# Moving one held store from GpSimd's queue to SyncE's, and counting with sixteen semaphores in place of thirty-six

## The chip, the cores and the metric

The kernel runs on one core of a Trainium2 chip. The metric is the device time of one execution in microseconds; the median of several executions is given, and beside it one execution that was profiled. The core's engines each run their own list of instructions: PE is TensorE (matrix products and transposes; PEld its weight loads), DVE is VectorE, ACT is ScalarE, POOL is GpSimd, SP is SyncE. They meet only through semaphores: an instruction can wait until a semaphore has reached a value, and can add to one when it is done. Transfers between the device memory and the core's on-chip memory are issued by GpSimd (queue q0, software_dynamic) or by SyncE (queue q1, hardware_dynamic), and are carried out by 16 DMA engines. A transfer adds 16 to its semaphore when all of it has landed. PSUM is the memory that TensorE writes, in eight banks.

## The reference

For each of 8 x 12 heads, a 1024 x 1024 matrix of weights is multiplied with a 1024 x 64 matrix:

```python
batch, n_heads, seq, head_dim = 8, 12, 1024, 64
attn_weights = np.random.randn(batch, n_heads, seq, seq).astype(np.float32)
v = np.random.randn(batch, n_heads, seq, head_dim).astype(np.float32)
return np.einsum('bhqs,bhsd->bhqd', attn_weights, v).astype(np.float32)
```

The weights are 403 MB in fp32, v and the output 25 MB each.

## The kernel before

**Units.** The 96 heads are taken four at a time (NV = 24 quartets, numbered q), and each quartet in two units (NU = 48, numbered n), each with half of the rows of the weights. A unit's weights are loaded in one transfer by GpSimd (`load_attn`, L340), which turns fp32 into bf16 on the way: 4 MB land in one of two buffers `abf`. The last two units' loads are cut into two halves each. v is loaded by GpSimd in a few larger pieces (`load_v`, L348), except for one part that SyncE loads at the start (L133).

**A unit on TensorE** (`pe_unit`, L198). It waits for its load, then transposes 16 groups g of the weights (`transpose_g`, L138, four matrix instructions each) into four PSUM banks in turn; group g goes to bank g % 4, and from g = 4 on has to wait until the copy of group g - 4 has emptied the bank. At g = 8 it also waits on `s_half`. In the first unit of a quartet it then spreads v over the partitions (`spread_v`, L153). `transpose_back` (L170) turns the products of the unit before; then come the products of this unit, 64 matrix instructions in two parts (`multiply`, L183), behind a wait on `s_last` for the last copies (L221).

**VectorE and ScalarE** (`engine`, L241, once for each). They share the 16 copies of the transposed groups out of PSUM (`copy_g`, L274: groups with g % 8 in 0, 2, 4, 5, 7 on VectorE, the others on ScalarE), the copies of spread v (`spread_copy`, L247), and the copies of the products into `ot` (`product`, L285). The copies of what was turned back into the output buffer `osb` (`back_copies`, L267) are ScalarE's, except for half of the last ones, which is VectorE's. A loop of 12 passes handles four units in each; the counts that a copy waits for are sums of a base in a register and a constant.

**GpSimd's list** (L365 to L402). Two loads at the start, two fills of constants (`affine_select`, L370 and L381), then for each unit n: wait until TensorE has transposed unit n's last group, then issue the load of unit n + 2 into the freed buffer (L395, L396). Behind the first units of quartets 8 and 16, it issues stores of finished output (`BURSTS`, L398: quartets 0 to 7, 8 and 9, 10 to 13). Then come the *held* stores (L400): quartets 14 and 15, 16 and 17, 18 and 19, one store of 2 MB for each pair, issued behind the last load in the same queue. Last stands `pool.drain()` (L402).

**SyncE's list** (L408 to L429). It relays landings to other engines: it waits for a burst or a load of v, then raises `s_free`, `s_half` or `s_vr`. At the end it waits for each of the two second half loads (L424), raising `s_half` (L425), then issues the store of quartets 20 and 21 (L427), waits until the last two copies into `osb` are done (`s_fin`, L428), and issues the last store, quartets 22 and 23 (L429).

**The end.** ScalarE, behind its copies, waits until GpSimd's held stores have landed (L335). All engines then meet (L135 in the profile: GpSimd gives the sign when it is through its list), ScalarE waits until SyncE's stores have landed (L432) and adds to the semaphore (L433), and the program clears its semaphores and ends (L459 in the profile).

**Semaphores.** There are 36: among them one for each of the groups 0 to 11 (`s_cp`, L125), `s_last` for groups 14 and 15, and for TensorE's work five: two for the transposes (`s_t`, by the engine that copies them), `s_sp` for spread v, `s_back` for what was turned back, `s_m` for the products.

Of the kernel before, what the change touches and what calls it, by code (L numbers as in the profile page):

```python
# [10 lines left out]
def kernel(  # L11
# [27 lines left out]
    VH = 4  # L39
# [14 lines left out]
    BY_SYNC = NV - 4  # L54
# [33 lines left out]
    def count_of(g):  # L88

        return sum(on_dve(x) == on_dve(g) for x in range(g + 1))  # L90

    PER_DVE = sum(on_dve(g) for g in range(G))
    PER_ACT = G - PER_DVE

# [40 lines left out]
    with tc.tile_critical(sync_engine=mybir.EngineType.Pool, no_gpsimd_drain=True):  # L135
        pe = nc.tensor

        def transpose_g(a, g, n):  # L138
            if g >= 4:
                pe.wait_ge(s_cp[g - 4], n)  # L140
            words = a[:, g].bitcast(fp32).rearrange("p (c k) -> p k c", k=KW)
            for k in range(KW):
                last = pe.matmul(  # L143
                    out=pt[g % 4][:, k],
                    lhsT=words[:, k],
                    rhs=ident,
                    is_transpose=True,
                    start=(k == 0),
                    stop=(k == KW - 1),
                )  # L150
            last.then_inc(s_t[on_dve(g)])

        def spread_v(n, banks):  # L153

            for pair in ((0, 2), (1, 3)):
                for b in range(VB):
                    for h in pair:
                        j = n % 2 * VH + h
                        rows = ds(j * (P // V8) // VR * VR, VR)
                        last = pe.matmul(  # L160
                            out=banks[h],
                            lhsT=spread[rows, j, ds(VB - 1 - b, P)],
                            rhs=vr[rows, n // 2, b],
                            start=(b == 0),
                            stop=(b == VB - 1),
                        )
                        if b == VB - 1:
                            last.then_inc(s_sp)

        def transpose_back():  # L170
            for j0 in range(0, GH, 4):
                for j in range(4):
                    last = pe.matmul(  # L173
                        out=px[j0 // 4][:, ds(j * P, P)],
                        lhsT=ot[:, j0 + j],
                        rhs=ident,
                        is_transpose=True,
                        start=(j == 0),
                        stop=(j == 3),
                    )  # L180
                last.then_inc(s_back)
# [16 lines left out]
        def pe_unit(i, n, both, loaded, it):  # L198

            pe.wait_ge(*loaded)  # L200
            for g in range(G):
                if g == GH:
                    pe.wait_ge(s_half, n)
                transpose_g(abf[i], g, n)
            pe.wait_ge(s_ot, both)
            if i == 0:
                pe.wait_ge(s_vr, it)
# [12 lines left out]
            transpose_back()  # L220
            pe.wait_ge(s_last, both)  # L221
            for hp in range(2):
                for h in range(2):
                    for half in range(2):
                        outs = po[hp][ds(half * D, D), ds(h * GH * VP, GH * VP)]
                        last = multiply(outs, 2 * hp + h, half)
                last.then_inc(s_m)

        pe.wait_ge(s_const, 4)
        with nc.Fori(1, NV + 1, 1, engines=(PE,)) as it:  # L230
# [4 lines left out]
            pe_unit(0, first, pe.snap(both - 2), (s_abf[0], loaded), it)  # L235
            pe_unit(1, second, both, (s_abf[1], loaded), it)
        pe.wait_ge(s_ot, 2 * (NU + 1))
# [3 lines left out]
        def engine(dve):  # L241
            eng = nc.vector if dve else nc.scalar
            copy = nc.vector.tensor_copy if dve else nc.scalar.copy
            per = PER_DVE if dve else PER_ACT
            e = 0 if dve else 1

            def spread_copy(h, ps, count):  # L247
                eng.wait_ge(s_sp, count)
                copy(  # L249
                    out=vbf[:, :, h], in_=ps.rearrange("p (k d) -> p k d", k=SB)  # L250
                ).then_inc(s_vbf)

            def back_copy(rows, n, k, count):

                eng.wait_ge(s_back, count)
                for pp in range(2):
                    last = copy(  # L257
                        out=rows[ds(n // 2 % 2 * HP, HP), ds(pp * 2 * G + n % 2 * G, G)].rearrange(
                            "p (half j) d -> p j half d", half=2
                        )[:, ds(4 * k, 4)],  # L260
                        in_=px[k][ds(pp * HP, HP)].rearrange(
                            "p (j half d) -> p j half d", half=2, d=D
                        ),
                    )
                return last

            def back_copies(rows, n, count, free=None):  # L267
                if free is not None:
                    eng.wait_ge(s_free, free)
# [4 lines left out]
            def copy_g(g, count):  # L274
                eng.wait_ge(s_t[dve], count)
                ins = copy(  # L276
                    out=at[:, g].rearrange("c k j two -> c (k j two)"),
                    in_=bank[g % 4].bitcast(bf16),
                )
                if g < G - 4:  # L280
                    ins.then_inc(s_cp[g])
                elif g == (G - 1 if dve else G - 2):
                    ins.then_inc(s_last)

            def product(count):  # L285

                eng.wait_ge(s_m, count)
# [7 lines left out]
            def unit(n, base, rows, free):  # L295

                of_t, of_sp, of_back, of_m = base
                for g in mine:
                    copy_g(g, of_t + (n * per + count_of(g)))
                if n % 2 == 0:  # L300
                    spread_copy(e, po[e], of_sp + (2 * n + 2 * e + 2))
                    spread_copy(2 + e, px[e], of_sp + (2 * n + 2 * e + 2))
                if not dve:
                    back_copies(rows, (n - 1) % un, of_back + 2 * n, free)
                product(of_m + (2 * n + e + 1))
# [3 lines left out]
            with nc.Fori(1, NU // un + 1, 1, engines=(DVE if dve else ACT,)) as it:  # L309
                base = [eng.snap(it * (un * k) - un * k) for k in (per, 2, 2, 2)]  # L310
# [3 lines left out]
                else:  # L314
                    now = eng.snap((it - 1) % (NO // 2))
                    before = eng.snap((it + (NO // 2 - 2)) % (NO // 2))
                    free = eng.snap(it + 0)
# [4 lines left out]
            back_copy(osb[:, slot(NV - 1)], NU - 1, k, 2 * NU + k + 1).then_inc(s_fin)  # L322

        nc.vector.memset(ident, 0.0).then_inc(s_const)  # L324
        nc.vector.memset(spread, 0.0).then_inc(s_const)
# [6 lines left out]
        last.then_inc(s_cast)  # L332
        engine(True)
        engine(False)
        nc.scalar.wait_ge(s_held, 16 * (BY_SYNC - HELD_FROM) // 2)  # L335
# [4 lines left out]
        def load_attn(n):  # L340
            pieces = [(0, G)] if n < HALVED else [(0, GH), (GH, GH)]
            for g0, gn in pieces:
# [3 lines left out]
                ).then_inc(s_abf[n % 2] if g0 == 0 else s_second[n], 16)  # L346
# [15 lines left out]
        def store_2(q):  # L362
            store(q, 2, pool, s_held)

        load_attn(0)  # L365
        pool.dma_start(out=vr_first[:, 1], in_=v_first[:, 1]).then_inc(s_v0, 16)
        load_attn(1)
        tc.wait_critical_data_deps()
        pool.wait_ge(s_const, 2)
# [8 lines left out]
        ).then_inc(s_const)  # L378

        pool.wait_ge(s_const, 3)  # L380
# [8 lines left out]
        ).then_inc(s_const)  # L389
        for n in range(NU - 2):  # L390
            q, i = n // 2, n % 2
            if i == 0 and q + 1 in V_LOADS:
                pool.wait_ge(s_sp, 4 * (q + 1))
# [14 lines left out]
        nc.sync.sem_inc(s_free, NO // 2)  # L408
        nc.sync.sem_inc(s_half, WHOLE[0])
        nc.sync.wait_ge(s_cast, 1)  # L410
        nc.sync.wait_ge(s_v0, 16)
        nc.sync.sem_inc(s_vr, 2)
        for k in range(1, NV // 2):
            stored = 2 * (k - 1)
            if stored in BURSTS:
                done = list(BURSTS).index(stored)
                nc.sync.wait_ge(s_osb, 16 * sum(len(BURSTS[x]) for x in BURSTS if x <= stored))
                nc.sync.sem_inc(s_free, sum(fours for _, fours in BURSTS[stored]) // 2)
                nc.sync.sem_inc(s_half, WHOLE[done + 1])  # L419
            if 2 * k in V_LOADS:  # L420
                nc.sync.wait_ge(s_v, 16 * (1 + list(V_LOADS).index(2 * k)))
# [9 lines left out]
        nc.scalar.reg_mov(landed, 16 * 2)  # L431
# [32 lines left out]
```

## Time and profile before

| | us |
|---|---|
| median of 3 runs | 1054.05 |
| lowest and highest of them | 1053.57, 1055.65 |
| the profiled execution | 1053.05 |
| its span, from the first to the last instruction | 1051.3 |
| mean granted clock of TensorE in it | 0.871 of full speed |

In the profile, times count from the start of the span. An engine's busy time leaves out what only its sequencer does: register instructions, branches, waits, the issuing of transfers; such rows carry a q (POOLq, SPq). A row of a group gives the line of the kernel, the engine, the operation, what is written and read, the count, then busy time, mean duration in ns and idle time before it. A row that asks for one line's instructions gives the shortest, median and longest duration in ns, then the first and last start in us. A row of waits gives who waited for whom: us in total, how often, the longest.

### The profile page before, as it was taken

To read this page: it belongs to the slowest core of one execution; us is meant where nothing else is said; L and a number is where in the kernel's file an instruction comes from. 1 tells how busy PE (TensorE), PEld (TensorE's weight loads), DVE (VectorE), ACT (ScalarE), POOL (GpSimd) and SP (SyncE) were. 2 spreads that over 40 slices of the span, in tenths; PEclk is the share of its full clock that TensorE was granted. 3 is DMA by queue.
4 is the path that set the end of the run, shared out by engine and by line. 5 is a ranking of instruction groups with operands and counts; after the bars stand their busy time and mean duration, and the time that the engine had idled before them with its cause. 6 is when DMAs were issued, how large, how long until landed. Compare 5 with 4: busy or idle time off the path is not lost.

```text
span 1051.3 us, 17364 instructions
## 1 busy us (share of the span) xinstructions
PE 796.3 (76%) x7304; PEld 709.4 (67%) x7304; DVE 389.5 (37%) x584; ACT 469.9 (45%) x590; POOL 37.4 (4%) x69
## 2 busy tenths in 40 slices
PE   0877788479889493878939789749588894978993
PEld 0776687468778483767838688648567784867873
DVE  1443344234435141343514344324334341534442
ACT  0445355244545251454626355434335443544552
POOL 1000000000000000000000000000000000000100
PEclk9989799698989697888969899878878987988997
DMA  9999999999999999999999999999999999999998
GB/s 215 225 218 218 216 217 209 219 219 219 217 218 214 218 211 379 219 219 216 215 217 213 216 219 219 209 226 218 330 217 216 219 210 225 218 216 216 211 231 369
DMA packets 10662, 239.68 MB, mean 228 GB/s; under 512 B 1056, under 2 KB 1056, under 8 KB 1184
## 3 DMA queue, kind: packets, MB, share of 16 engines
q0 software_dynamic: 10224, 234.36, 99.2%
q1 hardware_dynamic: 432, 5.24, 1.2%
q8 instruction: 3, 0.05, 0.0%
q14 instruction: 3, 0.02, 0.0%
HBM read 427.82 MB, written 25.17 MB: 431 GB/s over the span
## 4 chain that ended last, share of the span: by engine, by line
DMA 71%; PE 26%; issue 1%; POOL 1%; ACT 0%; DVE 0%; ACTq 0%; SPq 0%; POOLq 0%
DMA abf<-in_attn_weights_dram 63%; PE bank L143 22%; DMA out_dram<-osb 8%; PE bank L160 3%; PE bank L188 1%; PE bank L173 0%; POOL vr L349 0%; ACT osb L257 0%; DVE osb L257 0%; ACT vbf L249 0%; POOL abf L343 0%; ACT ot L288 0%; POOL out_dram L357 0%; ACTq L257 0%; SPq L419 0%
## 5 line engine op out<-in xcount | busy, mean ns | idle before, releaser
L143 PE MATMUL bank<-ident,abf 128*128 128x128 f32 x3072 | 431.5, 308 | 209.7 <-DMA abf<-in_attn_weights_dram 185.7
L143 PEld LDWEIGHTS bank<-ident,abf 128*128 128x128 f32 x3072 | 421.9, 212 | 221.4 <-DMA abf<-in_attn_weights_dram 193.0
L276 DVE COPY at<-bank 128x1024 bf16<-128x1024 bf16 x480 | 319.7, 689 | 401.0 <-PE bank L143 395.7
L276 ACT COPY at<-bank 128x1024 bf16<-128x1024 bf16 x288 | 288.0, 1013 | 327.8 <-PE bank L143 327.8
L188 PE MATMUL bank<-at,vbf 128*64 128x256 bf16 x3072 | 225.6, 285 | 0.0
L188 PEld LDWEIGHTS bank<-at,vbf 128*64 128x64 bf16 x3072 | 203.5, 111 | 19.4 <-issue 6.3
L257 ACT COPY osb<-bank 64x512 f32 (+1 forms) x194 | 112.5, 580 | 28.4 <-PE bank L173 25.7
L288 DVE COPY ot<-bank 128x512 f32<-128x512 f32 x48 | 33.2, 692 | 208.1 <-PE bank L188 208.1
L160 PE MATMUL bank<-vr,spread 32*128 32x512 bf16 x768 | 87.0, 375 | 0.5 <-issue 0.3
L288 ACT COPY ot<-bank 128x512 f32<-128x512 f32 x48 | 28.1, 586 | 129.7 <-PE bank L188 129.7
L173 PE MATMUL bank<-ident,ot 128*128 128x128 f32 x392 | 62.2, 311 | 29.4 <-ACT vbf L249 28.7
L173 PEld LDWEIGHTS bank<-ident,ot 128*128 128x128 f32 x392 | 51.1, 159 | 41.4 <-ACT vbf L249 40.5
L160 PEld LDWEIGHTS bank<-vr,spread 32*128 32x128 bf16 x768 | 35.0, 93 | 44.0 <-issue 1.6
L249 ACT CAST vbf<-bank 128x512 bf16<-128x512 f32 x48 | 25.8, 589 | 74.3 <-PE bank L160 74.3
L343 POOL DMA_DIRECT2D abf<-in_attn_weights_dram x50 | 26.9, 537 | 814.7 <-PE bank L143 813.8
L249 DVE CAST vbf<-bank 128x512 bf16<-128x512 f32 x48 | 30.9, 686 | 29.0 <-PE bank L160 29.0
L276 ACT ACT_TABLE_LOAD x12 | 15.4, 1283 | 6.6 <-DMA osb<-in_v_dram 6.5
L349 POOL DMA_DIRECT2D vr<-in_v_dram x6 | 4.0, 674 | 134.3 <-PE bank L160 134.3
L357 POOL DMA_DIRECT2D out_dram<-osb x6 | 3.6, 604 | 7.6 <-ACT osb L257 7.6
L324 DVE MEMSET ident<- 128x128 f32 x1 | 0.2, 165 | 6.4 <-DMA osb<-in_v_dram 6.4
L257 DVE COPY osb<-bank 64x512 f32<-64x512 f32 x2 | 1.4, 690 | 3.0 <-PE bank L173 3.0
L331 DVE CAST vr<-osb 128x1024 bf16<-128x1024 f32 x2 | 2.2, 1138 | 0.0
(9 smaller groups left out, 5.1 us busy)
## 6 DMA issues: line engine op xcount, KB each, us to landing
abf<-in_attn_weights_dram POOLq DMA_DIRECT2D x46, 4096.0 KB, 28.9
vr<-in_v_dram POOLq DMA_DIRECT2D x5, 2048.0 KB, 15.7
out_dram<-osb POOLq DMA_DIRECT2D x1, 8192.0 KB, 39.6
out_dram<-osb POOLq DMA_DIRECT2D x4, 2048.0 KB, 37.1
abf<-in_attn_weights_dram POOLq DMA_DIRECT2D x4, 2048.0 KB, 23.0
out_dram<-osb POOLq DMA_DIRECT2D x1, 4096.0 KB, 41.7
out_dram<-osb SPq DMA_DIRECT2D x2, 2048.0 KB, 12.9
osb<-in_v_dram SPq DMA_DIRECT2D x1, 1024.0 KB, 5.3
```

The costliest lines, as they stand in the source:

```text
L143: last = pe.matmul(out=pt[g % 4][:, k], lhsT=words[:, k], rhs=ident, is_transpose=True, start=(k == 0), stop=(k == KW - 1),)
L160: last = pe.matmul(out=banks[h], lhsT=spread[rows, j, ds(VB - 1 - b, P)], rhs=vr[rows, n // 2, b], start=(b == 0), stop=(b == VB - 1),)
L173: last = pe.matmul(out=px[j0 // 4][:, ds(j * P, P)], lhsT=ot[:, j0 + j], rhs=ident, is_transpose=True, start=(j == 0), stop=(j == 3),)
L188: last = pe.matmul(out=outs, lhsT=vbf[:, 2 * kw + par, h], rhs=at[:, ds(half * GH, GH), kw, ds(h * VP, VP), par], start=(n == 0), stop=(n ...
L249: copy(out=vbf[:, :, h], in_=ps.rearrange("p (k d) -> p k d", k=SB)).then_inc(s_vbf)
L257: last = copy(out=rows[ds(n // 2 % 2 * HP, HP), ds(pp * 2 * G + n % 2 * G, G)].rearrange("p (half j) d -> p j half d", half=2)[:, ds(4 * k ...
L276: ins = copy(out=at[:, g].rearrange("c k j two -> c (k j two)"), in_=bank[g % 4].bitcast(bf16),)
L288: copy(out=ot.rearrange("c j (pp h p) -> c h j pp p", pp=2, h=VH)[:, ds(2 * e, 2)], in_=po[e].rearrange("c (h j p pp) -> c h j pp p", h=2, ...
L331: last = nc.vector.tensor_copy(out=vr_first[:, 0, part], in_=v32[:, part])
L343: pool.dma_start(out=abf[n % 2][:, ds(g0, gn)].rearrange("p g s -> p (g s)"), in_=attn_q[n // 2][:, ds((n % 2 * G + g0) * S, gn * S)],).th ...
L349: pool.dma_start(out=vr[:, ds(q % V_AT_ONCE // 2, fours // 2)].rearrange("p n b x -> p n (b x)"), in_=v_n(q, fours),).then_inc(s_v, 16)
L357: eng.dma_start(out=out_n(q, fours), in_=at_slot, **({"single_packet": True} if eng is pool and fours == 2 else {}),).then_inc(done, 16)
```

## The change

- `BY_SYNC` is NV - 6 in place of NV - 4, and SyncE's one store behind the half loads becomes a loop. So the held store of quartets 18 and 19 is issued by SyncE, ahead of that of 20 and 21. Its landing counts on `s_end`, for which ScalarE now waits for three stores at the very end.
- GpSimd's held stores (now two) count on `s_osb`, the semaphore of the bursts, and GpSimd waits for the bursts before it issues them.
- One semaphore `s_pe` counts all that TensorE finishes in program order: transposed groups, spread v, what was turned back, products. `event` and `back_event` give the count at which something is done; a pair of units has EV = 44 such events.
- Each bank of the transposes has a semaphore (`s_bank`), which every copy out of it raises; TensorE waits for the count of that bank, held in registers, and before the products for all four banks.
- The remaining semaphores are merged in the same way: constants and VectorE's first cast count on `s_ot` and `s_vr`, the last copies on `s_vbf`, the freeing of output slots on `s_half`, the first load of v and the second half of unit 46's load on `s_v`.
- GpSimd's second fill of constants no longer waits for the first.

```diff
-    BY_SYNC = NV - 4
+    BY_SYNC = NV - 6
...
-    s_second = {n: sem(f"s_second{n}") for n in range(HALVED, NU)}
-    s_v0, s_v, s_cast = sem("s_v0"), sem("s_v"), sem("s_cast")
-    s_osb = sem("s_osb")
-    s_held, s_end = sem("s_held"), sem("s_end")
-
-    s_t = {True: sem("s_t_dve"), False: sem("s_t_act")}
-    s_sp, s_m = sem("s_sp"), sem("s_m")
-    s_back = sem("s_back")
-
-    s_cp = [sem(f"s_cp{g}") for g in range(G - 4)]
-    s_last, s_ot, s_vbf = sem("s_last"), sem("s_ot"), sem("s_vbf")
-
-    s_out, s_fin = sem("s_out"), sem("s_fin")
-    s_const, s_vr = sem("s_const"), sem("s_vr")
-
-    s_half, s_free = sem("s_half"), sem("s_free")
+    s_v, s_osb, s_end, s_second = sem("s_v"), sem("s_osb"), sem("s_end"), sem("s_second")
+
+    s_bank = [sem(f"s_bank{b}") for b in range(4)]
+    s_ot, s_vbf, s_out = sem("s_ot"), sem("s_vbf"), sem("s_out")
+
+    s_pe = sem("s_pe")
+
+    s_vr, s_half = sem("s_vr"), sem("s_half")
+
+    EV_BACK = (G + VH, 2 * G + VH + 4)
+    EV_UNIT = (0, G + VH + 4)
+    EV = 2 * (G + 4) + VH
+
+    def event(n, at):
+
+        return n // 2 * EV + EV_UNIT[n % 2] + at
+
+    def back_event(n, at):
+        return n // 2 * EV + EV_BACK[n % 2] + at
...
-        def transpose_g(a, g, n):
+        def transpose_g(a, g, copied):
             if g >= 4:
-                pe.wait_ge(s_cp[g - 4], n)
+                pe.wait_ge(s_bank[g % 4], copied[g // 4 - 1])
...
-            last.then_inc(s_t[on_dve(g)])
+            last.then_inc(s_pe)
...
-            pe.wait_ge(s_last, both)
+            for b in range(4):
+                pe.wait_ge(s_bank[b], copied[3])
...
-        pe.wait_ge(s_const, 4)
+        pe.wait_ge(s_vr, 3)
         with nc.Fori(1, NV + 1, 1, engines=(PE,)) as it:
...
+            copies = [pe.snap(it * 8 - 8 + k) for k in range(1, 9)]
+            pe_unit(0, first, both, (s_abf[0], loaded), it, copies[:4])
+            pe_unit(1, second, pe.snap(both + 2), (s_abf[1], loaded), it, copies[4:])
...
             def copy_g(g, count):
-                eng.wait_ge(s_t[dve], count)
-                ins = copy(
+                eng.wait_ge(s_pe, count)
+                copy(
                     out=at[:, g].rearrange("c k j two -> c (k j two)"),
                     in_=bank[g % 4].bitcast(bf16),
-                )
-                if g < G - 4:
-                    ins.then_inc(s_cp[g])
-                elif g == (G - 1 if dve else G - 2):
-                    ins.then_inc(s_last)
+                ).then_inc(s_bank[g % 4])
...
-        nc.scalar.wait_ge(s_held, 16 * (BY_SYNC - HELD_FROM) // 2)
+        nc.scalar.wait_ge(s_osb, 16 * (sum(len(x) for x in BURSTS.values()) + (BY_SYNC - HELD_FROM) // 2))
...
         def store_2(q):
-            store(q, 2, pool, s_held)
+            store(q, 2, pool, s_osb)
...
-            pool.wait_ge(s_t[True], (n + 1) * PER_DVE)
+            pool.wait_ge(s_pe, event(n, G))
             load_attn(n + 2)
...
+        pool.wait_ge(s_osb, 16 * sum(len(x) for x in BURSTS.values()))
         for q in range(HELD_FROM, BY_SYNC, 2):
             store_2(q)
         pool.drain()
...
         for n in range(HALVED, NU):
-            nc.sync.wait_ge(s_second[n], 16)
+            nc.sync.wait_ge(*second_of(n))
             nc.sync.sem_inc(s_half)
         nc.sync.wait_ge(s_osb, 16 * sum(len(x) for x in BURSTS.values()))
-        store(NV - 4, 2, nc.sync, s_end)
-        nc.sync.wait_ge(s_fin, 2)
+        for q in range(BY_SYNC, NV - 2, 2):
+            store(q, 2, nc.sync, s_end)
+        nc.sync.wait_ge(s_vbf, NV * VH + 2)
         store(NV - 2, 2, nc.sync, s_end, NU)
         landed = nc.scalar.alloc_register("landed")
-        nc.scalar.reg_mov(landed, 16 * 2)
+        nc.scalar.reg_mov(landed, 16 * (NV - BY_SYNC) // 2)
```

More of the change, by code (lines that the diff above doesn't have):

```diff
@@ L86, in on_dve @@
         return g % 8 in (0, 2, 4, 5, 7)
[L88 to L93, printed above, removed]
     sem = tc.alloc_semaphore
@@ L115, with second_of @@
     s_abf = [sem(f"s_abf{i}") for i in range(2)]
[L116 to L131 removed]
+    s_v, s_osb, s_end, s_second = sem("s_v"), sem("s_osb"), sem("s_end"), sem("s_second")
[10 more added lines that the diff above has]
+        return n // 2 * EV + EV_BACK[n % 2] + at
+    def second_of(n):
+        return (s_v, 16 * (2 + len(V_LOADS))) if n == HALVED else (s_second, 16)
     nc.sync.dma_start(out=v32, in_=v_first[:, 0])
@@ L167, in spread_v @@
                         if b == VB - 1:
-                            last.then_inc(s_sp)
+                            last.then_inc(s_pe)
         def transpose_back():
@@ L180, in transpose_back @@
                     )
-                last.then_inc(s_back)
+                last.then_inc(s_pe)
         def multiply(outs, h, half):
@@ L196, in multiply, with pe_unit @@
             return last
-        def pe_unit(i, n, both, loaded, it):
+        def pe_unit(i, n, both, loaded, it, copied):
             pe.wait_ge(*loaded)
@@ L203, in pe_unit @@
                     pe.wait_ge(s_half, n)
-                transpose_g(abf[i], g, n)
+                transpose_g(abf[i], g, copied)
             pe.wait_ge(s_ot, both)
             if i == 0:
-                pe.wait_ge(s_vr, it)
+                pe.wait_ge(s_vr, pe.snap(it + 3))
                 which = pe.snap((it - 1) % V_AT_ONCE)
@@ L226, in pe_unit @@
                         last = multiply(outs, 2 * hp + h, half)
-                last.then_inc(s_m)
-        pe.wait_ge(s_const, 4)
+                last.then_inc(s_pe)
+        pe.wait_ge(s_vr, 3)
         with nc.Fori(1, NV + 1, 1, engines=(PE,)) as it:
@@ L234 @@
             both = pe.snap(it * 4)
-            pe_unit(0, first, pe.snap(both - 2), (s_abf[0], loaded), it)
-            pe_unit(1, second, both, (s_abf[1], loaded), it)
-        pe.wait_ge(s_ot, 2 * (NU + 1))
+            copies = [pe.snap(it * 8 - 8 + k) for k in range(1, 9)]
+            pe_unit(0, first, both, (s_abf[0], loaded), it, copies[:4])
+            pe_unit(1, second, pe.snap(both + 2), (s_abf[1], loaded), it, copies[4:])
+        pe.wait_ge(s_ot, 2 * (NU + 2))
         transpose_back()
@@ L295, in unit @@
             def unit(n, base, rows, free):
-                of_t, of_sp, of_back, of_m = base
                 for g in mine:
-                    copy_g(g, of_t + (n * per + count_of(g)))
+                    copy_g(g, base + event(n, g + 1))
                 if n % 2 == 0:
-                    spread_copy(e, po[e], of_sp + (2 * n + 2 * e + 2))
-                    spread_copy(2 + e, px[e], of_sp + (2 * n + 2 * e + 2))
+                    spread_copy(e, po[e], base + event(n, G + 2 * e + 2))
+                    spread_copy(2 + e, px[e], base + event(n, G + 2 * e + 2))
                 if not dve:
-                    back_copies(rows, (n - 1) % un, of_back + 2 * n, free)
-                product(of_m + (2 * n + e + 1))
+                    back_copies(rows, (n - 1) % un, base + back_event(n, 0), free)
+                product(base + back_event(n, 2 + e + 1))
             un = 4
             with nc.Fori(1, NU // un + 1, 1, engines=(DVE if dve else ACT,)) as it:
-                base = [eng.snap(it * (un * k) - un * k) for k in (per, 2, 2, 2)]
+                base = eng.snap(it * (un // 2 * EV) - un // 2 * EV)
                 if dve:
@@ L321, in engine @@
             k = 1 - e
-            back_copy(osb[:, slot(NV - 1)], NU - 1, k, 2 * NU + k + 1).then_inc(s_fin)
-        nc.vector.memset(ident, 0.0).then_inc(s_const)
-        nc.vector.memset(spread, 0.0).then_inc(s_const)
+            back_copy(osb[:, slot(NV - 1)], NU - 1, k, NU // 2 * EV + k + 1).then_inc(s_vbf)
+        nc.vector.memset(ident, 0.0).then_inc(s_ot)
+        nc.vector.memset(spread, 0.0).then_inc(s_ot)
         for h in range(2):
@@ L331 @@
             last = nc.vector.tensor_copy(out=vr_first[:, 0, part], in_=v32[:, part])
-        last.then_inc(s_cast)
+        last.then_inc(s_vr)
         engine(True)
         engine(False)
-        nc.scalar.wait_ge(s_held, 16 * (BY_SYNC - HELD_FROM) // 2)
+        nc.scalar.wait_ge(s_osb, 16 * (sum(len(x) for x in BURSTS.values()) + (BY_SYNC - HELD_FROM) // 2))
         pool = nc.gpsimd
@@ L345, in load_attn @@
                     in_=attn_q[n // 2][:, ds((n % 2 * G + g0) * S, gn * S)],
-                ).then_inc(s_abf[n % 2] if g0 == 0 else s_second[n], 16)
+                ).then_inc(s_abf[n % 2] if g0 == 0 else second_of(n)[0], 16)
         def load_v(q, fours):
@@ L362, in store_2 @@
         def store_2(q):
-            store(q, 2, pool, s_held)
+            store(q, 2, pool, s_osb)
         load_attn(0)
-        pool.dma_start(out=vr_first[:, 1], in_=v_first[:, 1]).then_inc(s_v0, 16)
+        pool.dma_start(out=vr_first[:, 1], in_=v_first[:, 1]).then_inc(s_v, 16)
         load_attn(1)
         tc.wait_critical_data_deps()
-        pool.wait_ge(s_const, 2)
+        pool.wait_ge(s_ot, 2)
         pool.affine_select(
@@ L377 @@
             channel_multiplier=1,
[L378 to L380 removed]
+        ).then_inc(s_vr)
         pool.affine_select(
@@ L388 @@
             channel_multiplier=VB,
-        ).then_inc(s_const)
+        ).then_inc(s_vr)
         for n in range(NU - 2):
@@ L402 @@
         pool.drain()
-        nc.sync.sem_inc(s_free, NO // 2)
         nc.sync.sem_inc(s_half, WHOLE[0])
-        nc.sync.wait_ge(s_cast, 1)
-        nc.sync.wait_ge(s_v0, 16)
+        nc.sync.wait_ge(s_vr, 3)
+        nc.sync.wait_ge(s_v, 16)
         nc.sync.sem_inc(s_vr, 2)
@@ L417 @@
                 nc.sync.wait_ge(s_osb, 16 * sum(len(BURSTS[x]) for x in BURSTS if x <= stored))
-                nc.sync.sem_inc(s_free, sum(fours for _, fours in BURSTS[stored]) // 2)
                 nc.sync.sem_inc(s_half, WHOLE[done + 1])
             if 2 * k in V_LOADS:
-                nc.sync.wait_ge(s_v, 16 * (1 + list(V_LOADS).index(2 * k)))
+                nc.sync.wait_ge(s_v, 16 * (2 + list(V_LOADS).index(2 * k)))
                 nc.sync.sem_inc(s_vr, V_LOADS[2 * k])
         for n in range(HALVED, NU):
-            nc.sync.wait_ge(s_second[n], 16)
+            nc.sync.wait_ge(*second_of(n))
             nc.sync.sem_inc(s_half)
         nc.sync.wait_ge(s_osb, 16 * sum(len(x) for x in BURSTS.values()))
-        store(NV - 4, 2, nc.sync, s_end)
-        nc.sync.wait_ge(s_fin, 2)
+        for q in range(BY_SYNC, NV - 2, 2):
+            store(q, 2, nc.sync, s_end)
+        nc.sync.wait_ge(s_vbf, NV * VH + 2)
         store(NV - 2, 2, nc.sync, s_end, NU)
         landed = nc.scalar.alloc_register("landed")
-        nc.scalar.reg_mov(landed, 16 * 2)
+        nc.scalar.reg_mov(landed, 16 * (NV - BY_SYNC) // 2)
     tc.keep_in_program_order(nc.scalar.wait_ge(s_end, nc.scalar.snap(landed)))
```

13 lines of the change are left out of this document (6 added, 7 removed).

## The prediction

> **What bounds the kernel now.** I first read how busy the engines and the DMA queues are over the whole span.
>
> ```profile
> span 1051.3 us, 17364 instructions
> PE 796.3 (76%) x7304; PEld 709.4 (67%) x7304; DVE 389.5 (37%) x584; ACT 469.9 (45%) x590; POOL 37.4 (4%) x69
> DMA  9999999999999999999999999999999999999998
> q0 software_dynamic: 10224, 234.36, 99.2%
> q1 hardware_dynamic: 432, 5.24, 1.2%
> ```
>
> The 16 DMA engines are busy in every slice, and the packets of the two queues (q0 is GpSimd's, q1 SyncE's) fill about 100% of 16 engines' span. No compute engine is above 76%. Then the stretches; the columns are stretch, its length, busy time of PE, PEld, DVE, ACT and POOL, granted clock, busy share of the DMA engines, GB/s.
>
> ```profile
> 100.00:200.00 100.00, 66.93 (x618) 59.90 (x619) 32.58 (x49) 41.09 (x52) 2.85 (x5) 0.85 1.01 217
> 900.00:1000.00 100.00, 87.42 (x820) 77.67 (x817) 40.92 (x62) 51.32 (x66) 5.27 (x10) 0.90 1.00 216
> ...
> 1024.00:1028.00 4.00, 3.26 (x27) 3.26 (x28) 2.49 (x4) 2.37 (x3) 0.00 (x0) 1.00 1.02 434
> 1028.00:1032.00 4.00, 4.00 (x52) 3.77 (x51) 1.43 (x3) 3.33 (x5) 0.00 (x0) 1.00 0.99 422
> 1032.00:1036.00 4.00, 3.23 (x41) 2.67 (x36) 0.75 (x2) 1.08 (x2) 0.00 (x0) 1.00 1.01 434
> 1036.00:1040.00 4.00, 0.00 (x0) 0.00 (x0) 1.32 (x2) 0.67 (x2) 0.00 (x0) 0.98 0.99 422
> 1040.00:1044.00 4.00, 0.00 (x0) 0.00 (x0) 0.00 (x0) 0.00 (x0) 0.00 (x0) 0.50 1.02 438
> 1044.00:1046.00 2.00, 0.00 (x0) 0.00 (x0) 0.00 (x0) 0.00 (x0) 0.00 (x0) 0.50 0.98 418
> 1046.00:1048.00 2.00, 0.00 (x0) 0.00 (x0) 0.00 (x0) 0.00 (x0) 0.00 (x0) 0.50 0.79 336
> 1048.00:1049.00 1.00, 0.00 (x0) 0.00 (x0) 0.00 (x0) 0.00 (x0) 0.00 (x0) 0.50 0.04 16
> ...
> 1048.25:1048.50 0.25, 0.00 (x0) 0.00 (x0) 0.00 (x0) 0.00 (x0) 0.00 (x0) 0.50 0.00 0
> ```
>
> The DMA share is 1.0 while loads run, and still about 1.0 from 1024 to 1046, when only stores are left. PE is finished by 1036, yet bytes move until about 1048.3. So the end of the data is set by the sum of the bytes, not by any wait. Between that and the end of the span lie some 3 us without traffic. For those I read the stores one by one (start, then time from issue to landing), the sequencers' own instructions (durations min/median/max in ns, then when), and SyncE's waits.
>
> ```profile
> L357 POOL DMA_DIRECT2D out_dram<-osb x3: 532/544/544, 997.7 to 998.8; - x3
> DMA to landing us min/median/max: 33.1/41.1/48.5
> ...
> L357 SPq DMA_DIRECT2D out_dram<-osb x1: 342/342/342, 1024.8 to 1024.8; - x1
> DMA to landing us min/median/max: 14.1/14.1/14.1
> ...
> L357 SPq DMA_DIRECT2D out_dram<-osb x1: 332/332/332, 1037.4 to 1037.4; - x1
> DMA to landing us min/median/max: 11.7/11.7/11.7
> ...
> L431 ACTq MOVE  x1: 29/29/29, 1047.2 to 1047.2; - x1
> L402 POOLq DRAIN  x1: 51390/51390/51390, 998.4 to 998.4; - x1
> SPq L135 <- POOLq L135: 12.2, 1, 12.2
> L433 ACTq EVENT_SEMAPHORE  x1: 17/17/17, 1050.1 to 1050.1; - x1
> ```
>
> GpSimd's three held stores land at about 1030.8, 1039.3 and 1047.3 (998.8 + 48.5); SyncE's land at 1038.9 and, last of all, 1049.1 (1037.4 + 11.7). But GpSimd's drain lasts until 998.4 + 51.4 = 1049.8, and SyncE, done issuing at 1037.7, waits 12.2 us for GpSimd, to 1049.9. Only behind that does ScalarE reach its wait for the last store, which has been fulfilled for 1.0 us: it goes through at 1050.1, and the span ends 1.2 us later. So the last thing that the end waits for is GpSimd's drain, 2.5 us behind the landing of GpSimd's own last store.
>
> **The change, part by part.** *The store.* Store 18 (2048 KB) leaves the end of GpSimd's queue and stands in SyncE's, behind the wait for the last half load and ahead of store 20. GpSimd loses one DMA issue (0.54 us, at 998.8, with nothing of GpSimd's own behind it but the drain); SyncE gains one (0.34 us, at 1024.8). Store 20 then goes out at about 1025.2, and nothing but SyncE's wait for the last copies, which ends at 1037.4, is queued behind it. The bytes are the same and the engines have no idle time to win or lose, so the data still end just after 1048 and the last store lands near 1049.1, provided that the engines always have work queued. At 1037.4, when the last store is issued, they do: the five stores are 5 x 2.097 = 10.5 MB; at some 430 GB/s the last one takes 4.9 us, so that its bytes are not needed before 1048.3 - 4.9 = 1043.4. How long SyncE's queue takes to start is bounded by its load at the beginning of the kernel:
>
> ```profile
> osb<-in_v_dram SPq DMA_DIRECT2D x1, 1024.0 KB, 5.3
> ```
>
> 1.05 MB at 430 GB/s are 2.4 us, which leaves at most 2.9 us for start and completion (estimate from these rows). The last store is ready by 1040.3, with 3.1 us to spare. That the two queues share evenly I take from the landings: SyncE's first store and GpSimd's second land within 0.4 us of each other (1038.9 and 1039.3). So GpSimd's second store, then its last, still lands near 1039.3.
>
> What the move frees is the drain. If it follows GpSimd's own landings at the same distance, it ends at 1039.3 + 2.5 = 1041.8, all engines meet by 1042, and ScalarE waits for the last store itself: through at 1049.1, plus the 1.2 us behind, gives a span of 1050.3 in place of 1051.3. That is the term: **-1.0 us**. Its bounds: 0 if the drain follows something else, -1.6 if the last store also lands 0.6 us earlier, which the last rival below allows.
>
> The Trainium skill, "DMA: Bandwidth & Descriptors", section "Issuing engines are not separate DMA queues", speaks against any gain: transfers from SyncE and GpSimd run on the same 16 engines, and another issuing engine saves only sequencer time. The trace agrees for the data (422 to 438 GB/s whichever queues are filled); by that rule alone the sum would be 0 and not -1.0, which is the first rival below.
>
> *The counters.* One counter of TensorE's events takes the place of five, four bank counters that of thirteen, and constants become sums in registers. The order of instructions on each engine stays; in TensorE's loop body of two units nine register instructions are added, and before each unit's products it waits for four counters in place of one, three waits more. Prices from the nearest rows of the same sequencer:
>
> ```profile
> L230 PEldq ALU_OP  x24: 36/36/42, 60.0 to 1032.6; - x24
> L140 PEldq EVENT_SEMAPHORE  x48: 51/51/51, 30.6 to 1023.2; - x48
> ```
>
> 9 x 36 + 6 x 51 = 630 ns for two units, 15 us over 24 passes if nothing hid it. What hides it is the lead of the loads:
>
> ```profile
> POOL abf L343 <- PE bank L143: 813.8, 40, 34.0
> PE bank L143 <- DMA abf<-in_attn_weights_dram: 185.7, 26, 25.4
> ...
> DMA to landing us min/median/max: 27.7/28.9/47.1
> ```
>
> The last row is of the loads between 20 and 960 us. A load of 4.19 MB takes 19.3 us at 217 GB/s and lands 27.7 us after its issue at the least, so it is issued at least 8.4 us before the engines need it. A unit that is 0.3 us later delays the next issue by 0.3 of these 8.4 us. TensorE itself idles 186 us for loads. I take 0; the bounds are 0 and 15 us, and the value lies at the end that the DMA share of 1.0 shows. In the tail, where no load is left, the additions between the last half load and the last store are three register instructions and three waits, 0.26 us: the last store goes out at 1037.7, against the 3.1 us to spare. ScalarE's loop body of four units has nine rows more; ScalarE is busy 45%, and its copies lie under the same lead.
>
> *The start.* TensorE now also starts behind VectorE's cast (L331), and the second fill of the constants no longer waits for the first.
>
> ```profile
> L331 DVE CAST vr<-osb x2: 629/1138/1647, 8.7 to 9.3; 128x1024 bf16<-128x1024 f32 x2
> L143 PE MATMUL bank<-ident,abf x3072: 272/283/491, 25.4 to 1028.6; 128*128 128x128 f32 x192
> ```
>
> The cast is done at 10.9, TensorE's first matmul waits for its data until 25.4: nothing. GpSimd's new wait ahead of the held stores asks for bursts that were stored long before; behind it stand only the held stores and the drain, and those stores can't move before the loads ahead of them in the queue. Nothing.
>
> *Clearing at the end.* One instruction clears the semaphores:
>
> ```profile
> L459 POOLq EVENT_SEMAPHORE_RANGE_CLEAR  x1: 268/268/268, 1050.7 to 1050.7; - x1
> ```
>
> If its time goes by their number, 16 in place of 36 save 0.15 us; if it is fixed, none. I take none.
>
> The sum: 0 for the data, -1.0 at the end, 0 for the rest. The profiled execution took 1053.05 us, 1.75 us around its span, and lies 1.0 us below the median of the runs shown, 1054.05. Against itself it would come to 1052.05; against the median, 1053.05.
>
> **The rivals.** *The drain is not freed (0 us, 1054.05).* It might wait until nothing is in flight on any queue, or something else of GpSimd's might hold it: it ends only 0.7 us after SyncE's last landing, which is as close as one expects of a direct follower, and 2.5 us after GpSimd's own, which is far. Against it: the drain belongs to GpSimd's instruction stream, where only its own transfers stand. The same result comes if the join of the engines takes its time elsewhere; then the change doesn't do what it seems to.
>
> *SyncE's queue can't keep the engines filled alone (slower).* In the profile before, GpSimd's queue holds work until 1047.3, so no row shows SyncE's queue carrying the engines through two stores by itself. From 1039.3 it must. If each store there started only when the one before had landed, store 20 would begin at 1038.9 and take 2.9 + 4.9 us, to 1046.7, and the last to 1054.5: 5.4 us later than 1049.1. The span is then 1054.5 + 1.2 = 1055.7, 4.4 us more than before, and the time 1058.5. It decides as soon as the idle time exceeds the 1.0 us won. Against it: the last store was issued at 1037.4 with the first still in flight (to 1038.9), and the rate never fell below 418 GB/s up to 1046; GpSimd's stores land 8 us apart without a gap.
>
> *TensorE's additions come through.* Up to +15 us, if a unit's lead were gone; it would take over 8.4 us of delay in one unit, against 0.3.
>
> *The engines finish more evenly (faster).* From 1046 to 1048 the rate sinks from 418 to 336 GB/s, and 16 in the next: some engines are done earlier. The 0.69 MB of these stretches at 430 GB/s would be over at 1047.6, up to 0.6 us sooner than now; with the drain freed too, 1052.4.
>
> **How the numbers follow.** Forecast 0.62; drain not freed 0.25; SyncE's queue 0.07; TensorE 0.03; evener 0.03. Some 0.2% (2.1 us) is what a measurement of this kernel tells from no change: the three runs alone span 2.1 us. The two likeliest cases lie within it, at -0.1% and 0; to either side I give room for the spread of medians and for the cases beyond. So faster 0.13, same 0.74, slower 0.13. The predicted time is 1053.0. The range takes in both likely cases with 1.4 us below the first (the bound of -1.6 included) and 1.6 above the second, the highest run: 1051.6 to 1055.6. SyncE's rival and TensorE's stay outside.
>
> **What would show it.** Drain: its end some 2.5 us behind 1039, ScalarE's last wait ending with the last landing. If the drain still ends near 1049.8, the first rival holds. Data: a DMA share of 1.0 to 1046, two GpSimd landings near 1031 and 1039, SyncE's near 1049; a hole after 1039 is the second rival. Counters: the largest gap of the DMA share in any stretch up to 1020 stays nil, and the last store is issued between 1037.4 and 1037.9. The prediction is wrong if the last byte moves by over 1 us, or the time by over 2.

## The result, and the profile after

| | before | changed |
|---|---|---|
| median of 18 runs, us | 1053.16 | 1051.80 |
| lowest and highest, us | 1052.64, 1055.65 | 1051.28, 1052.19 |
| the profiled execution, us | 1053.05 | 1051.49 |
| its span, us | 1051.3 | 1049.7 |

The ratio of changed to before is 0.9985, with a 95% interval of 0.9978 to 0.9991: some 0.15% faster, within the 0.2% that the prediction called no change, but clear of no change in this measurement.

First the stretches of the changed kernel (columns as before: stretch, length, PE, PEld, DVE, ACT, POOL, granted clock, DMA share, GB/s).

```profile
100.00:200.00 100.00, 71.30 (x647) 63.34 (x642) 33.24 (x50) 41.24 (x52) 2.85 (x5) 0.83 1.01 216
900.00:1000.00 100.00, 88.45 (x840) 78.45 (x837) 41.26 (x62) 51.33 (x66) 4.76 (x9) 0.91 1.00 215
...
1024.00:1028.00 4.00, 3.42 (x28) 3.42 (x29) 2.52 (x5) 2.23 (x3) 0.00 (x0) 1.00 1.02 438
1028.00:1032.00 4.00, 4.00 (x52) 3.72 (x53) 1.26 (x2) 3.33 (x5) 0.00 (x0) 1.00 0.99 422
1032.00:1036.00 4.00, 3.11 (x38) 2.55 (x35) 0.87 (x2) 1.19 (x3) 0.00 (x0) 1.00 1.01 434
1036.00:1040.00 4.00, 0.00 (x0) 0.00 (x0) 1.20 (x2) 0.56 (x1) 0.00 (x0) 0.66 1.00 426
1040.00:1044.00 4.00, 0.00 (x0) 0.00 (x0) 0.00 (x0) 0.00 (x0) 0.00 (x0) 0.50 1.02 434
1044.00:1046.00 2.00, 0.00 (x0) 0.00 (x0) 0.00 (x0) 0.00 (x0) 0.00 (x0) 0.50 1.01 434
1046.00:1048.00 2.00, 0.00 (x0) 0.00 (x0) 0.00 (x0) 0.00 (x0) 0.00 (x0) 0.50 0.69 295
```

The data are as they were: a DMA share of about 1 up to 1046 (0.92 from 1020 to 1024, where the kernel before has 0.93), 422 to 438 GB/s in the tail to 1046, and no hole after 1040, from where SyncE's queue is the only one with work. The difference lies behind them. Here are GpSimd's and SyncE's stores (count, durations in ns, start; then issue to landing in us), and the sequencers' instructions at the end.

```profile
L352 POOL DMA_DIRECT2D out_dram<-osb x2: 544/544/544, 996.4 to 996.9; - x2
DMA to landing us min/median/max: 34.2/38.8/43.4
...
L352 SPq DMA_DIRECT2D out_dram<-osb x1: 332/332/332, 1037.2 to 1037.2; - x1
DMA to landing us min/median/max: 11.6/11.6/11.6
...
L397 POOLq DRAIN  x1: 46096/46096/46096, 996.8 to 996.8; - x1
SPq L134 <- POOLq L134: 5.4, 1, 5.4
L427 ACTq EVENT_SEMAPHORE  x1: 17/17/17, 1048.8 to 1048.8; - x1
L453 POOLq EVENT_SEMAPHORE_RANGE_CLEAR  x1: 160/160/160, 1049.2 to 1049.2; - x1
```

GpSimd's last store now lands at 996.9 + 43.4 = 1040.3, and its drain ends at 996.8 + 46.1 = 1042.9, 2.6 us behind it; before it was 2.5 us behind 1047.3. SyncE waits 5.4 us for GpSimd in place of 12.2. ScalarE gets to its last wait early and goes through at 1048.8, when SyncE's last store lands (1037.2 + 11.6). Before, that store had landed 1.0 us ahead of ScalarE. From there to the end of the span it is 0.9 us in place of 1.2.

### The profile page after: what moved, and what is told of

It is laid out like the page before. It is cut to its first block, busy times and chain, and to the rows that moved or that the text cites. A ratio compares the mean times of both kernels' runs of the same rounds, so it can differ in the third digit from the quotient of the medians.

```text
span 1049.7 us, 17710 instructions
## 1 busy us (share of the span) xinstructions
PE 793.8 (76%) x7304; PEld 706.7 (67%) x7304; DVE 389.3 (37%) x584; ACT 469.8 (45%) x590; POOL 37.0 (4%) x68
## 4 chain that ended last, share of the span: by engine, by line
DMA 71%; PE 26%; issue 1%; POOL 1%; ACT 0%; DVE 0%; ACTq 0%; SPq 0%; POOLq 0%
DMA abf<-in_attn_weights_dram 63%; PE bank L142 22%; DMA out_dram<-osb 8%; PE bank L159 3%; PE bank L187 1%; PE bank L172 0%; POOL vr L344 0%; ACT osb L257 0%; DVE osb L257 0%; ACT vbf L249 0%; POOL abf L338 0%; ACT ot L284 0%; POOL out_dram L352 0%; ACTq L257 0%; SPq L412 0%
## 5 line engine op out<-in xcount | busy, mean ns | idle before, releaser
L172 PE MATMUL bank<-ident,ot 128*128 128x128 f32 x392 | 61.1, 307 | 29.3 <-ACT vbf L249 28.7
## 6 DMA issues: line engine op xcount, KB each, us to landing
abf<-in_attn_weights_dram POOLq DMA_DIRECT2D x46, 4096.0 KB, 29.3
```

The source lines that it names most:

```text
L172: last = pe.matmul(out=px[j0 // 4][:, ds(j * P, P)], lhsT=ot[:, j0 + j], rhs=ident, is_transpose=True, start=(j == 0), stop=(j == 3),)
```

## The experiments

Three theories stood against each other. By the drain theory the end waits for the later of two things: GpSimd's drain, some 2.6 us behind GpSimd's own last landing, and SyncE's last landing. By the counter theory the gain comes from the counters. The queue theory has SyncE's queue carry the tail's data better than GpSimd's.

**The store alone** (e1_store_only): the kernel before, with

```diff
-    BY_SYNC = NV - 4
+    BY_SYNC = NV - 6
...
-        store(NV - 4, 2, nc.sync, s_end)
+        for q in range(BY_SYNC, NV - 2, 2):
+            store(q, 2, nc.sync, s_end)
...
-        nc.scalar.reg_mov(landed, 16 * 2)
+        nc.scalar.reg_mov(landed, 16 * (NV - BY_SYNC) // 2)
```

> The kernel before with store 18 moved to SyncE's queue and nothing else; the thirty-six semaphores stay. Drain theory (GpSimd's drain ends some 2.6 us behind the landing of GpSimd's own last store, and the end waits for the later of that drain and SyncE's last landing): the drain ends near 1043 in place of 1049.8, ScalarE's last wait ends with SyncE's last landing near 1049, the clearing stays at 0.27 us, and the span comes to 1050.1 to 1050.4: 0.9 to 1.2 us faster than before, most of the changed kernel's gain. Counter theory (the gain comes from the counters and the shorter clearing): within 0.3 us of before.

Measured: 1051.67 us against 1052.94 of the kernel before on the same chip, ratio 0.9987 (0.9978 to 0.9996). The rows are the drain, ScalarE's passing of GpSimd's held stores, its last wait, and the clearing.

```profile
span 1050.2 us, 17364 instructions
L402 POOLq DRAIN  x1: 45718/45718/45718, 997.3 to 997.3; - x1
L432 ACTq MOVE  x1: 29/29/29, 1040.5 to 1040.5; - x1
L434 ACTq EVENT_SEMAPHORE  x1: 17/17/17, 1049.2 to 1049.2; - x1
L460 POOLq EVENT_SEMAPHORE_RANGE_CLEAR  x1: 268/268/268, 1049.6 to 1049.6; - x1
```

GpSimd's stores land at 1040.5, the drain ends at 1043.0, ScalarE's last wait at 1049.2. The store's move alone brings 1.3 us of the changed kernel's 1.4, with the thirty-six semaphores in place. The move takes one thing more with it: the kernel gives the option `single_packet` only to GpSimd's two-quartet stores, so the moved store loses it. No run separates the two; two later readings speak against a part of the option in the gain (the drain behind a load, in the run with all five on SyncE's queue, and the length of the tail, in the account of the prediction).

**The counters alone** (e2_counters_only): the changed kernel, with

```diff
-    BY_SYNC = NV - 6
+    BY_SYNC = NV - 4
```

> The changed kernel with store 18 back on GpSimd's queue: the counters alone. Drain theory: the drain ends near 1049.7 again and the end waits for it; only the clearing is shorter (0.16 in place of 0.27 us), so 0.1 to 0.4 us faster than before. Counter theory: 1.0 to 1.5 us faster than before, as the changed kernel.

Measured: 1052.75 us against 1052.94, ratio 0.9997 (0.9988 to 1.0006).

```profile
span 1050.7 us, 17710 instructions
L397 POOLq DRAIN  x1: 51101/51101/51101, 998.3 to 998.3; - x1
L425 ACTq MOVE  x1: 29/29/29, 1046.8 to 1046.8; - x1
L427 ACTq EVENT_SEMAPHORE  x1: 17/17/17, 1049.6 to 1049.6; - x1
L453 POOLq EVENT_SEMAPHORE_RANGE_CLEAR  x1: 160/160/160, 1050.2 to 1050.2; - x1
```

The drain ends at 1049.4 again, 2.6 us behind the landing at 1046.8, and ScalarE's last wait ends behind it. The counters are worth 0.19 us by the medians, which the interval can't tell from nothing; 0.11 us of it can be seen, in the clearing (268 to 160 ns). All 11 runs, 1052.35 to 1053.09 us, lie above all 11 of the store alone on the same chip, 1051.45 to 1052.00. The counter theory falls.

**Forty spare semaphores** (e5_spare_sems): the changed kernel, with

```diff
+    spare = [sem(f"s_spare{i}") for i in range(40)]
```

> The changed kernel with forty spare semaphores that nothing uses, fifty-six in all. If the clearing at the end goes by their number (0.268 us with thirty-six, 0.160 us with sixteen: 5.4 ns each), it takes 0.16 + 40 x 0.0054 = 0.38 us and the span is 0.2 us longer than the changed kernel's; if the number plays no part, it stays at 0.16 us.

```profile
span 1049.8 us, 17710 instructions
L454 POOLq EVENT_SEMAPHORE_RANGE_CLEAR  x1: 377/377/377, 1049.1 to 1049.1; - x1
```

The clearing took 377 ns where 0.38 us were forecast: 160, 268 and 377 ns for 16, 36 and 56 semaphores lie on one line, 5.4 ns for each. The whole time, 1051.59 us in one run, lies in the changed kernel's spread, and one run can't show the forecast 0.2 us.

**No drain, before** (e3_no_drain): the kernel before, with

```diff
-        pool.drain()
```

> The kernel before without GpSimd's drain at the end of its list; all stores and semaphores as before. Drain theory: GpSimd gives its sign when its last issue is done, near 999, and the engines meet once ScalarE has seen GpSimd's held stores land, near 1047.3; then ScalarE waits for SyncE's last landing near 1049 and the span is 1050.1 to 1050.5, 0.8 to 1.2 us faster than before, with no store moved. Queue theory (SyncE's queue carries the tail's data better): no gain, within 0.3 us of before.

Measured: 1055.33 us against 1052.94, ratio 1.0023 (1.0014 to 1.0032). Both theories missed. The group of the program's own drains on GpSimd shows why (three of them; the longest 5.2 us, the first at 1047.4):

```profile
span 1053.6 us, 17363 instructions
L458 POOLq DRAIN  x3: 51/131/5205, 1047.4 to 1053.3; - x3
L432 ACTq EVENT_SEMAPHORE  x1: 17/17/17, 1049.1 to 1049.1; - x1
```

The engines do meet near 1047.3 as forecast, and ScalarE's last wait ends with SyncE's landing at 1049.1. But the program itself drains GpSimd three times at its end, which took 39 to 131 ns each in the kernel before. With the kernel's drain left out, the first of the three has the whole work to do: from 1047.4 to 1052.6.

**Landed, then drained** (e9_landed_then_drain): the kernel before, with

```diff
+        pool.wait_ge(s_held, 16 * (BY_SYNC - HELD_FROM) // 2)
         pool.drain()
```

> The kernel before with a wait in GpSimd's list, until its three held stores have landed, ahead of its drain. If the drain has 5.2 us of work of its own that it can otherwise do in part while stores are in flight, it starts near 1047.3 and lasts 5.2 us, and the span is near 1053.7. If it just ends 2.6 us behind the last landing, it lasts 2.6 us and the span stays near 1051.3.

```profile
span 1053.6 us, 17364 instructions
L403 POOLq DRAIN  x1: 5205/5205/5205, 1047.0 to 1047.0; - x1
```

It lasts 5.2 us although the stores have landed when it begins, and the span is that of the kernel before without its drain (one run, 1055.39 us against 1052.75). So a drain behind these transfers has 5.2 us to do; begun while stores are in flight, it has 2.5 to 2.7 us left when the last one lands. What GpSimd does in that time no row shows.

**No drain, changed** (e8_changed_no_drain): the changed kernel without `pool.drain()`.

> The changed kernel without GpSimd's drain at the end of its list. In the kernel before, leaving it out moved its work to the program's own drain, which then took 5.2 us from the landing of GpSimd's last store. Here that would start near 1040.4 and be over near 1045.6, before SyncE's last landing at 1048.8: within 0.3 us of the changed kernel. If instead the program's drain waits for SyncE's transfers or follows the last landing by 2.6 us or more, the span is 2 us longer or worse.

Measured: 1051.61 us against 1053.01, ratio 0.9984 (0.9975 to 0.9994), as the changed kernel.

```profile
span 1049.9 us, 17709 instructions
L452 POOLq DRAIN  x3: 46/108/5127, 1040.7 to 1049.7; - x3
L426 ACTq EVENT_SEMAPHORE  x1: 17/17/17, 1049.0 to 1049.0; - x1
```

The drain now runs from 1040.7 to 1045.8, under SyncE's stores. The same instruction, left out in the same way, costs 2.4 us in the kernel before and nothing here: it is the order of the two ends that counts.

**One held store on GpSimd's queue** (e7_one_held_store_on_pool): the changed kernel with `BY_SYNC = NV - 8`.

> The changed kernel with one held store on GpSimd's queue and four stores on SyncE's. Drain theory: the drain ends still earlier (2.6 us behind a landing near 1029), the end waits for SyncE's last landing as in the changed kernel, and one store of GpSimd's, 4.9 us of work, covers SyncE's start: within 0.4 us of the changed kernel. Queue theory: faster than the changed kernel by about 1 us again.

Measured: 1051.41 us against 1053.01, ratio 0.9986 (0.9977 to 0.9996).

```profile
span 1049.5 us, 17710 instructions
L352 POOL DMA_DIRECT2D out_dram<-osb x1: 544/544/544, 997.2 to 997.2; - x1
DMA to landing us min/median/max: 33.1/33.1/33.1
...
L397 POOLq DRAIN  x1: 35762/35762/35762, 997.1 to 997.1; - x1
L427 ACTq EVENT_SEMAPHORE  x1: 17/17/17, 1048.6 to 1048.6; - x1
```

GpSimd's one held store lands at 1030.3. The drain ends at 1032.9, 10 us sooner than in the changed kernel, and the span (1049.5) is the same within 0.2 us: with the drain out of the way nothing more is won. The queue theory would have had another microsecond.

**All five on SyncE's queue** (e4_all_sync): the changed kernel with `BY_SYNC = NV - 10`.

> The changed kernel with all five last stores on SyncE's queue, none of the held ones on GpSimd's. Drain theory: nothing more to win at the end, since the drain is early already; but SyncE issues its first store only when the last half load has landed, so the 16 DMA engines stand idle from about 1023 to 1024 until SyncE's first packets, some 3 us behind the issue near 1024.6: a DMA share well under 1 between 1024 and 1028, the last landing 3 to 4.5 us later, span 1052.5 to 1054.5. Queue theory: as fast as the changed kernel or faster.

Measured: 1053.75 us against 1052.94, ratio 1.0005 (0.9996 to 1.0015).

```profile
1022.00:1024.00 2.00, 2.00 (x18) 1.95 (x17) 1.73 (x3) 1.57 (x3) 0.00 (x0) 1.00 0.28 57
1024.00:1026.00 2.00, 1.11 (x10) 0.97 (x9) 0.90 (x3) 0.71 (x1) 0.00 (x0) 1.00 0.29 123
1026.00:1028.00 2.00, 2.00 (x19) 2.00 (x18) 1.46 (x3) 1.70 (x2) 0.00 (x0) 1.00 0.96 401
...
L397 POOLq DRAIN  x1: 31311/31311/31311, 996.1 to 996.1; - x1
L427 ACTq EVENT_SEMAPHORE  x1: 17/17/17, 1051.2 to 1051.2; - x1
```

The hole is there: with shares of 0.28 and 0.29, some 2.9 us of all engines are lost between 1022 and 1026, and the last landing comes at 1051.2, 2.4 us later than in the changed kernel. Some 0.4 of these are not the hole's: SyncE passed the last half load at 1024.9 in place of 1024.45, for a reason that no row shows. The delay is less than the 3 to 4.5 us expected (span 1052.1, forecast 1052.5 to 1054.5): SyncE's transfers reached 401 GB/s in the stretch from 1 to 3 us behind their first issue at 1025.0. In the packets of the trace the first one starts at 1025.9, 0.9 us behind the issue, where the expectation had some 3 us. SyncE's queue alone then filled the engines for some 24 us (a mean share of 1.00 and 426 GB/s from 1026 to 1050), so it is as good as GpSimd's but no better. GpSimd's last transfer is a load here, which landed at 1024.9 and has no `single_packet`; the drain ended at 1027.4, 2.5 us behind it.

**Only the last store on SyncE's queue** (e6_last_store_only_on_sync): the changed kernel with `BY_SYNC = NV - 2`.

> The changed kernel with four held stores on GpSimd's queue and the last one alone on SyncE's: one store more on GpSimd's queue than before the change. Drain theory, by the order of the bytes: GpSimd's queue has the engines alone until the last store's packets begin near 1040.5 and shares them after that; its last landing comes near 1046.3, the drain ends near 1048.9, about when SyncE's last store lands; span 1049.9 to 1050.6, 0.2 to 0.9 us above the changed kernel and 0.7 to 1.4 us below before. If only the number of stores on GpSimd's queue counted, it would be slower than before.

Measured: 1052.76 us against 1053.01, ratio 0.9997 (0.9987 to 1.0006): a miss by half a microsecond. It is no slower than before, though GpSimd has a store more, but gains only 0.25 us by the medians where 0.7 to 1.4 were expected.

```profile
span 1051.1 us, 17709 instructions
L397 POOLq DRAIN  x1: 50870/50870/50870, 999.0 to 999.0; - x1
L425 ACTq MOVE  x1: 29/29/29, 1047.2 to 1047.2; - x1
L427 ACTq EVENT_SEMAPHORE  x1: 17/17/17, 1050.1 to 1050.1; - x1
```

GpSimd's fourth store landed at 1047.2, not 1046.3 as I had worked out from an even sharing of the last stretch; the drain follows by 2.7 us as elsewhere (1049.9), and the end behind the drain.

## Why the prediction was right and wrong

*Right: the place and the mechanism.* The last thing the end waited for was GpSimd's drain, and moving the store took it off. Over eight kernels in which the drain began before the landing, it ended 2.5 to 2.7 us behind GpSimd's last landing, whether that was at 1025, 1030, 1040 or 1047, a store or a load, and whatever SyncE's queue did. That settles the rival by which the drain waits for all queues: in the changed kernel it ended 5.9 us ahead of SyncE's last landing (1042.9 and 1048.8).

*Right: the data and the three rivals that touch it.* No hole after 1040, so SyncE's stores don't wait for each other; the lead of the loads hides the counters' instructions (median from issue to landing 29.3 us, 28.9 before). The last store went out at 1037.2, not later than before. Nor do the engines finish more evenly. The rows have the moment when SyncE passes the last half load, before and changed:

```profile
1024.68 0.02 SPq L425
...
1024.45 0.02 SPq L418
```

From there to the last landing (1049.1 and 1048.8) it is 24.4 us in both, and 24.4 to 24.6 us in the eight other runs that leave a held store on GpSimd's queue. One bound was too low, without harm: for the start and completion of a SyncE transfer the sum allowed 2.9 us, from the load at the kernel's beginning. With the engines full, the first packet of SyncE's first store alone came 3.5 us behind its issue in the changed kernel (1024.6 to 1028.1), and 3.5 us behind the last store's issue in the run with only that store on SyncE's queue (1037.5 to 1041.0), still ahead of the 1043.4 at which the prediction needed its bytes.

The rule of the Trainium skill ("DMA: Bandwidth & Descriptors", "Issuing engines are not separate DMA queues") held for the bytes: the rates are the same whichever queue carries them (422 to 438 GB/s with both queues, a mean of 426 with SyncE's alone). By that rule alone the sum was 0; the store's move alone was worth 1.3 us, since GpSimd has a drain to finish behind its own transfers.

*Wrong: the size of the end.* The term was -1.0 us; the spans differ by 1.6 and the medians by 1.36. Two parts of it were mis-sized. "Plus the 1.2 us behind": behind ScalarE's last wait the profile after has 0.9 us. In the kernel before, part of the 1.2 was still the meeting of the engines, which now is over at 1043; with the store alone the part behind the wait is 1.0 (1049.2 to 1050.2). And "I take none" for the clearing: it goes by the number of semaphores, 0.11 us, near the 0.15 that I had as its bound. The rest, 0.2 to 0.3 us, is where the last store landed: 1048.8 in place of 1049.1. Since the tail behind the last half load is as long as before, this came from loads that ended 0.2 us sooner, not from the stores. The profiled executions scatter by more: SyncE passes the last half load between 1024.4 and 1024.7 in those with the old semaphores, and between 1024.2 and 1024.7 in those with the new ones and a held store on GpSimd's queue. Whether the counters have a small share in it stays open.

*Wrong: the level.* The sum was put on the median of three runs, 1054.05; over 18 runs before has 1053.16, close to its profiled execution. 0.9 of the 1.2 us between the predicted 1053.0 and the measured 1051.8 come from there.

*Wrong: what can be told from no change.* This is the step that turned a term of -1.0 us into a forecast of no change. I took the spread of three single runs, 2.1 us, for the resolution, and so gave "faster" 0.13 although the sum itself was -1.0 us. The interval over 18 runs is 0.07% to either side, and the gain lies outside it. A term that the trace shows with its sign, in a tail that hardly varies, deserved to be called a small gain, not no change.

## What to carry to other kernels

Where the DMA engines are full to the last byte, look at what each engine still has to do behind its own last transfer: the end is the later of these chains, and the transfer that finishes last should belong to the engine with the shortest one. Leave enough on the other queue to cover the time until the new queue's first transfer moves bytes. In the run with all stores on SyncE's queue nothing covered it: SyncE issues only behind its wait for the last half load, and 2.1 us were lost (median 1053.75 us, 1051.67 with the store alone on the same chip). An instruction that looks like pure waiting, such as the drain, may hold work that only turns up elsewhere when it is taken out.

## What the runs showed of the hardware

A drain of GpSimd behind its transfers takes 5.1 to 5.2 us when all of GpSimd's have landed before it begins (three runs), and ends 2.5 to 2.7 us behind the last landing when it begins earlier (eight); left out, its time appears in the program's own drain. The first packet of a SyncE transfer starts 0.9 us behind the issue when the 16 DMA engines are idle (1025.0 to 1025.9), and 3.5 us behind it when GpSimd's stores keep them full (1024.6 to 1028.1). Clearing semaphores at the end takes 160, 268 and 377 ns for 16, 36 and 56 of them, 5.4 ns each on top of some 74 ns.
